# A three-block network on one core: expert results written per choice and summed on VectorE, first gathers ahead of a branch, unread matmuls in TensorE's waits

## The chip, the core and the metric

The kernel runs on one core of a Trainium2 chip. A core has five engines that each work through their own queue in order: TensorE (PE in the profile; its weight loads are PEld), VectorE (DVE), ScalarE (ACT), GpSimd (POOL) and SyncE (SP), which here only issues DMAs. Sixteen DMA engines move data between the chip's memory and the core. The metric is the device time of one execution in microseconds.

## What is computed

One call takes 512 latent tokens of width 1024 and 256 context tokens through a first block (a mixer of two gated linear recurrences, `hg` and `dn`, then a mixture of experts) and a second block (attention, a convolutional feed-forward, a spatial gating unit, a second feed-forward), all in float32. The change touches the mixture of experts most:

```python
def hierarchical_moe(h, w_group, b_group, w_expert, b_expert, w_gate, w_up, w_down):
    t = h.reshape(-1, h.shape[-1])
    ...
    g_idx = jnp.argmax(g_logits, axis=-1)              # one group of 4 experts
    ...
    top_v, top_i = lax.top_k(e_in_group, TOP_K_IN_GROUP)   # two experts of it
    top_w = jax.nn.softmax(top_v, axis=-1) * g_w
    ...
    y = jnp.zeros_like(t)
    for e in range(N_EXPERTS):                         # 16
        a = jax.nn.silu(t @ w_gate[e]) * (t @ w_up[e])
        y = y + gates[:, e:e + 1] * (a @ w_down[e])
    return y.reshape(h.shape)
```

Every token has exactly two experts, a first and a second choice, with weights from the softmax.

## The kernel before

**Precision.** Each float32 operand of a large matmul is split into a high and a low part (`split`: a cast on ScalarE makes the high part, a subtraction on VectorE the low part), and three matmuls are added up (`mm3`): high x high, low x high, high x low. In the trace a weight tile arrives as `wraw` or `wrawx` (1 MB, 128x2048), and its parts are `whi` and `wlo` (128x1024, two pieces to a load). `load_raw` issues the load on SyncE's queue when a buffer is free: two `wraw` and, in the expert phase, four `wrawx`. Of `whi` and `wlo` there are four buffers each.

**Order.** The program is written as Python generators that are advanced by turns; a scheduler then fixes the order of each engine's queue before the kernel runs. An engine that waits holds up all that stands behind it in its queue. `issue_after` ties instructions to stand behind a given one on its engine.

**Before the experts.** The recurrences end in `hg_core` and `dn_core`; each is followed by a projection. `out_proj` multiplies 1024 features in 4 blocks, adds the result to the residual stream `x`, and, in halves of 256 tokens, takes the mean square of the new rows (`msq`: matmuls with `ones`; `pow_half` on GpSimd; `spread`: transposes of `rrt`). It is used after the recurrences (`w_out`), after the attention, in the feed-forwards and in the gating unit.

**Experts.** `moe` writes the normed tokens to the table `hd` in memory, works out router logits, the two choices (`e12`, `mmask`) and each token's position in its expert's list (`posm`). `slot_onehot` makes one-hot matrices `soh` for two experts at a time; `slot_rows` multiplies them with `tw` (token number, weight high, weight low), copies the product to `srs`, transposes it and works out an index `sri` and a weight `srw` for each of an expert's 128 slots. An empty slot points behind the 512 tokens. `gather_slots` fetches the 128 token rows `xt` with an indirect DMA on GpSimd's queue, and `slots_feature` turns them into `xghi` and `xglo`. An expert (`hidden`, `turned`, `down`) needs 6 MB of weights: gate, up (contracted over 1024), then `esg` and `ea` (128x512), their transposes split into `eahi` and `ealo`, then down. The result `ey` is added into the rows of the table `ysd` by an indirect DMA that accumulates (`compute_op=ALU.add`). `ysd` has been zeroed earlier by five DMAs. Experts with more than 128 tokens are worked off in a loop inside a branch (`moe_overflow`), whose condition each engine loads; in the profiled data the branch is not taken. Before the branch six weight loads are issued (`early`). `moe` also gets `fill`, one step of the modulation vectors (eight matmuls, `L355`).

`moe_add` reads `ysd` back (`ys`, four loads of 128x4x256), transposes it, adds it to `x` with a gate and sums the squares. During this time TensorE has matmuls of the attention's projections on the context and latent tokens (`hthi`) to do.

## Time and profile before

| | us |
|---|---|
| median of three runs | 2380.99 (2379.49 to 2387.99) |
| the profiled execution, its own time | 2387.35 |
| span of that execution's trace | 2385.5 |
| TensorE busy | 2240.5 (94%) |
| VectorE busy | 1614.3 (68%) |
| ScalarE busy | 1200.8 (50%) |
| GpSimd busy | 620.3 (26%) |

The mean granted TensorE clock is 0.972 of full speed. The page's chain of waits, followed back from the last instruction, lies on TensorE for its matmuls for the most part. The busy time of an engine is an average over stages with different limits, and a matmul's end is modelled, so a busy TensorE isn't one at its peak. What a place is worth is read from the views of that place: which engine idled there, and what ended the idle time.

### The profile page before, as it was taken

The numbers are of one execution on the slowest core, as the hardware profiler recorded it, in microseconds if no ns is written. First come the engines' busy times: TensorE is split into PE (matmuls) and PEld (weight loads), VectorE is DVE, ScalarE is ACT, GpSimd is POOL, SyncE is SP. The second block draws the span as 40 slices with busy tenths as digits, with TensorE's granted clock in tenths as the row PEclk, the third lists the DMA queues.
The fourth block names the chain that finished last, engine by engine and source line by source line (L and its number), as shares of the span: only waits on it lengthen the run. The fifth ranks groups of instructions, "written<-read, shape, count | busy, mean of one in ns | idle before, by whom it ended". The sixth has DMA issues, their size and how long they took to land.

```text
span 2385.5 us, 33834 instructions
## 1 busy us (share of the span) xinstructions
PE 2240.5 (94%) x13058; PEld 1880.5 (79%) x13058; DVE 1614.3 (68%) x2545; ACT 1200.8 (50%) x1969; POOL 620.3 (26%) x470
## 2 busy tenths in 40 slices
PE   6998989989988899999999999999999999999998
PEld 3988977758875677778778878878888988888887
DVE  4777877778855888886857865896673445553553
ACT  4455644456754677776337763432342433432433
POOL 2133544345421111100441422332333001110111
PEclk9999999999999899999999999999999999999999
DMA  8564004151045799997210002656433222323321
GB/s 317 186 222 143 28 1 153 46 219 74 2 177 230 281 395 368 372 379 267 77 39 1 2 36 107 237 193 231 148 131 102 102 89 71 106 73 113 106 74 60
DMA packets 68405, 355.24 MB, mean 149 GB/s; under 512 B 8065, under 2 KB 12817, under 8 KB 37009
## 3 DMA queue, kind: packets, MB, share of 16 engines
q1 hardware_dynamic: 62752, 333.94, 38.0%
q0 software_dynamic: 5488, 19.11, 3.3%
q8 instruction: 104, 1.70, 0.3%
q14 instruction: 61, 0.49, 0.1%
HBM read 334.45 MB, written 19.40 MB: 148 GB/s over the span
## 4 chain that ended last, share of the span: by engine, by line
PE 43%; DVE 5%; issue 1%; ACT 1%; DMA 0%; POOL 0%; SPq 0%; POOLq 0%; DVEq 0%; ACTq 0%
PE mm L531 12%; PE mm L532 12%; PE mm L530 12%; PE sc L1598 2%; PE av L1751 1%; PE aux L1616 1%; DVE mva L385 1%; PE av L1742 1%; DVE smax L1605 1%; DVE wlo L273 1%; PE aux L1587 0%; DVE cy L1868 0%; PE aux L388 0%; DVE st L1577 0%; DVE alo L273 0%
## 5 line engine op out<-in xcount | busy, mean ns | idle before, releaser
L530 PE MATMUL mm<-hhi,whi 128*128 128x512 f32 (+1 forms) x1184 | 438.0, 375 | 10.3 <-ACT whi L270 5.3
L531 PE MATMUL mm<-hlo,whi 128*128 128x512 f32 (+1 forms) x1184 | 441.5, 374 | 2.9 <-DVE hlo L482 2.9
L532 PE MATMUL mm<-hhi,wlo 128*128 128x512 f32 (+1 forms) x1184 | 438.7, 372 | 0.0
L270 ACT CAST whi<-wraw 128x1024 fp32r<-128x1024 f32 (+1 forms) x240 | 246.3, 1041 | 300.1 <-PE mm L531 223.5
L273 DVE TENSOR_TENSOR wlo<-wraw,whi 128x1024 fp32r<-128x1024 f32 (+1 forms) x203 | 249.3, 1244 | 179.9 <-ACT whi L270 179.1
L273 DVE TENSOR_TENSOR wlo<-wrawx,whi 128x1024 fp32r<-128x1024 f32 x190 | 229.0, 1230 | 94.3 <-ACT whi L270 93.0
L270 ACT CAST whi<-wrawx 128x1024 fp32r<-128x1024 f32 (+1 forms) x210 | 215.0, 1048 | 154.2 <-PE mm L531 106.1
L530 PEld LDWEIGHTS mm<-hhi,whi 128*128 128x128 f32 x1184 | 224.8, 191 | 49.4 <-ACT whi L270 5.9
L531 PEld LDWEIGHTS mm<-hlo,whi 128*128 128x128 f32 x1184 | 225.9, 191 | 41.5 <-DVE hlo L482 3.3
L532 PEld LDWEIGHTS mm<-hhi,wlo 128*128 128x128 f32 x1184 | 225.4, 191 | 38.0 <-issue 0.2
L530 PE MATMUL mm<-whi,hhi 128*128 128x512 f32 (+1 forms) x640 | 218.2, 346 | 6.3 <-ACT hhi L481 2.3
L532 PE MATMUL mm<-whi,hlo 128*128 128x512 f32 (+1 forms) x640 | 219.9, 347 | 3.8 <-DVE hlo L482 3.7
L531 PE MATMUL mm<-wlo,hhi 128*128 128x512 f32 (+1 forms) x640 | 219.6, 345 | 0.5 <-DVE wlo L273 0.4
L385 DVE SCALAR_TENSOR_TENSOR mva<-mvr,cc_c,mva 128x512 f32<-128x512 f32 x154 | 156.6, 1017 | 3.4 <-DMA mvr<-in_w_mod_dram 1.2
L1878 POOL TENSOR_TENSOR cy<-cy,csg 128x512 f32<-128x512 f32 x44 | 64.7, 1472 | 348.0 <-DVE cy L1870 332.5
L531 PE MATMUL mm<-alo,whi 128*128 128x512 f32 (+1 forms) x396 | 145.0, 366 | 0.0
L530 PE MATMUL mm<-ahi,whi 128*128 128x512 f32 (+1 forms) x396 | 144.7, 367 | 0.0
L532 PE MATMUL mm<-ahi,wlo 128*128 128x512 f32 (+1 forms) x396 | 144.4, 366 | 0.0
L273 POOL TENSOR_TENSOR wlo<-wraw,whi 128x1024 fp32r<-128x1024 f32 (+1 forms) x37 | 90.1, 2434 | 203.7 <-ACT whi L270 195.4
L530 PEld LDWEIGHTS mm<-whi,hhi 128*128 128x128 f32 x640 | 125.1, 196 | 20.3 <-ACT hhi L481 2.8
L532 PEld LDWEIGHTS mm<-whi,hlo 128*128 128x128 f32 x640 | 124.9, 196 | 19.7 <-DVE hlo L482 6.2
L531 PEld LDWEIGHTS mm<-wlo,hhi 128*128 128x128 f32 x640 | 125.0, 196 | 14.4 <-DVE wlo L273 1.3
(548 smaller groups left out, 4672.4 us busy)
## 6 DMA issues: line engine op xcount, KB each, us to landing
wrawx<-in_w_down_dram SPq DMA_DIRECT2D x32, 1024.0 KB, 9.1
wrawx<-in_w_gate_dram SPq DMA_DIRECT2D x30, 1024.0 KB, 9.0
wraw<-in_w_up_dram SPq DMA_DIRECT2D x30, 1024.0 KB, 9.2
wraw<-in_ffn_w_up_dram SPq DMA_DIRECT2D x30, 1024.0 KB, 4.8
mvr<-in_ada_w_dram SPq DMA_DIRECT2D x56, 512.0 KB, 4.5
wraw<-in_ada_w_dram SPq DMA_DIRECT2D x20, 1024.0 KB, 4.9
wraw<-in_w_in_dram SPq DMA_DIRECT2D x18, 1024.0 KB, 6.9
mvr<-in_w_mod_dram SPq DMA_DIRECT2D x32, 512.0 KB, 4.4
```

The costliest lines, as they stand in the source:

```text
L270: nc.scalar.copy(hi, src)
L273: (lo_eng or nc.vector).tensor_sub(lo, src, hi.bitcast(F32))
L385: nc.vector.scalar_tensor_tensor(acc, raw[:, k, :], c, acc, op0=ALU.mult, op1=ALU.add)
L530: nc.tensor.matmul(out, ahi, bhi, start=start, stop=False)
L531: nc.tensor.matmul(out, ahi, blo, start=False, stop=False)
L532: nc.tensor.matmul(out, alo, bhi, start=False, stop=stop)
L1598: nc.tensor.matmul(s[:, a:a + n], qs[:, qt * P:qt * P + P], ks[i][:, a:a + n], start=i == 0, stop=i == 1)
L1605: nc.vector.tensor_reduce(m, s[:, :768], axis=AX.X, op=ALU.max, negate=True)
L1616: nc.tensor.transpose(tp[:, j, :], p[:, (a + j) * P:(a + j + 1) * P], self.ident)
L1742: nc.tensor.matmul(av[:, qt, :], pt[:, k, :], hd["v"][:, k, :], start=k == 0, stop=k == 5)
L1751: nc.tensor.matmul(av[j * 64:j * 64 + 64, qt, :], hd["v"][:, k, :], pt[:, k, :], start=k == 0, stop=k == 5, tile_position=(0, j * 64))
L1878: nc.gpsimd.tensor_mul(y, y, sg)
```

## The change

1. `ysd` grows from 640 to 1152 rows. A token's first choice is written to its own row and its second choice to the row 512 further on, so that no row is written twice. `tw` gets a fourth column with that row number, `slot_rows` gives two indices (`srix` for the gather, `sriy` for the scatter), the scatter is a plain write, and the zeroing DMAs go. `moe_add` loads both halves (eight loads, two buffers for each half) and adds them on VectorE.
2. The slot rows of experts 0 and 1 and their two gathers stand ahead of the overflow branch. The step `fill` stands behind the matmul `pre`, later than before.
3. Eight early weight loads instead of six, and six `wrawx` buffers instead of four; in the branch one buffer instead of two.
4. `warm` puts matmuls of `ones` with a constant, 128x512 in float32, into TensorE's queue. Nobody reads the result. There are four at the end of `hg_core`, four at the end of `dn_core`, two behind the second mean square in `out_proj` (after the recurrences, the attention, the first feed-forward and the gating unit), five ahead of the branch, four behind the sums of `moe_add`, and one and two in the first transposes of the attention.

```diff
+    def warm(self, behind, n):
+        with self.tc.issue_after(behind.ins):
+            p = self.ps.tile([P, 512], F32, name="aux", tag="aux")
+            for _ in range(n):
+                self.nc.tensor.matmul(p, self.ones, self.wide, start=True, stop=True)
...
@@ out_proj
                     bs.append(self.rstd(acc, ts.start // P, 2))
+                    if ts.start and not end:
+                        self.warm(self.summed, 2)
@@ hg_core, finish
+            if h == 3:
+                self.warm(out, 4)
             self.head_out(cp, po, ox[:, :, h * P:h * P + P])
@@ dn_chunk
-            mm4(p2, qk, vn)
+            out = mm4(p2, qk, vn)
+            if last and d:
+                self.warm(out, 4)
@@ down
-        nc.gpsimd.indirect_dma_start(out=ysd, out_offset=bass.IndirectOffsetOnAxis(ap=slot[0], axis=0), in_=y,
-                                     in_offset=None, compute_op=ALU.add)
+        nc.gpsimd.indirect_dma_start(out=ysd, out_offset=bass.IndirectOffsetOnAxis(ap=slot[1], axis=0), in_=y,
+                                     in_offset=None)
@@ slot_rows
-            row = pool.tile([P, 1], I32, name=name + "ri", bufs=8)
-            nc.vector.scalar_tensor_tensor(row, v[:, 0:1], float(T), w[:, 1:2], op0=ALU.add, op1=ALU.add)
+            row = [pool.tile([P, 1], I32, name=name + "ri" + c, bufs=8) for c in "xy"]
+            for c in range(2):
+                nc.vector.scalar_tensor_tensor(row[c], v[:, c:c + 1], float(T + c * T), w[:, 1:2], op0=ALU.add, op1=ALU.add)
@@ moe
-        for _ in fill:
-            pass
-        mvstack.close()
...
+        pre = nc.tensor.matmul(p[:, 1, :], self.ones, mf, start=True, stop=True)
+        with tc.issue_after(pre.ins):
+            for _ in fill:
+                pass
...
+        ty = rp.tile([P, 4, 16], F32, name="ty")
+        nc.vector.tensor_scalar(ty, e12[:, 1], float(T), float(-T), op0=ALU.mult, op1=ALU.add)
+        nc.vector.tensor_add(tw[:, :, :, 1], ty, self.c["tok"].unsqueeze(2).to_broadcast([P, 4, 16]))
...
+        two_rows(0)
+        gather(0)
+        gather(1)
+        self.warm(self.rowed, 5)
...
-                      for n, e in (("w_gate", 0), ("w_up", 0), ("w_gate", 1)) for k0 in (0, 4)]
+                      for n, e in (("w_gate", 0), ("w_up", 0), ("w_gate", 1), ("w_up", 1)) for k0 in (0, 4)]
         self.moe_overflow(dp, hd, ysd, tw, posm, ovl)
...
-            two_rows(0)
-            gather(0)
-            gather(1)
@@ moe_add
-        ys = pool.tile([P, 4, D], F32, name="ys")
-        for c in range(4):
-            nc.sync.dma_start(ys[:, :, c * 256:c * 256 + 256],
-                              ysd[0:T, c * 256:c * 256 + 256].rearrange("(j p) c -> p j c", p=P))
         for k in range(KD):
+            if k % 2 == 0:
+                ys = [pool.tile([P, 4, 256], F32, name=f"ys{c}", bufs=2) for c in range(2)]
+                for c in range(2):
+                    nc.sync.dma_start(ys[c], ysd[c * T:c * T + T, k * P:k * P + 256].rearrange("(j p) c -> p j c", p=P))
+                nc.vector.tensor_add(ys[0], ys[0], ys[1])
...
+        self.warm(self.summed, 4)
@@ the first block
-                for j in range(5):
-                    nc.sync.dma_start(ysd[j * P:j * P + P, :], z)
...
-            with K.phase(5, 0, 4):
+            with K.phase(5, 0, 6):
```

The scheduler's order moves with it. VectorE's queue around the fifth `srs` (the slot rows of experts 8 and 9; `xglo` is the low part of an expert's gathered rows; numbers tell buffers apart), before:

```order
L273 TENSOR_TENSOR xglo_9490<-aux_9491,xghi_9489 128x512
L273 TENSOR_TENSOR xglo_9490<-aux_9498,xghi_9489 128x512
L1325 COPY srs_9513<-aux_9508 6x256
L1245 TENSOR_TENSOR soh_9870<-cst_69,posm_8228 128x4x128
L273 TENSOR_TENSOR wlo_9447<-wrawx_9444,whi_9446 128x1024
L1245 TENSOR_TENSOR soh_9870<-cst_69,posm_8228 128x4x128
L1333 TENSOR_SCALAR srw_9518<-aux_9515,cst_69 128x1
L273 TENSOR_TENSOR wlo_9451<-wrawx_9444,whi_9450 128x1024
```

and with the change:

```order
L273 TENSOR_TENSOR xglo_9532<-aux_9533,xghi_9531 128x512
L273 TENSOR_TENSOR xglo_9532<-aux_9540,xghi_9531 128x512
L273 TENSOR_TENSOR wlo_9493<-wrawx_9486,whi_9492 128x1024
L273 TENSOR_TENSOR wlo_9512<-wrawx_9509,whi_9511 128x1024
L273 TENSOR_TENSOR wlo_9516<-wrawx_9509,whi_9515 128x1024
L1343 COPY srs_9555<-aux_9550 8x256
L1262 TENSOR_TENSOR soh_9916<-cst_69,posm_8243 128x4x128 x2
L273 TENSOR_TENSOR wlo_9577<-wrawx_9574,whi_9576 128x1024
L273 TENSOR_TENSOR wlo_9581<-wrawx_9574,whi_9580 128x1024
L273 TENSOR_TENSOR wlo_9605<-wraw_9602,whi_9604 128x1024
```

Three `wlo` that stood behind `srs` and `soh` now stand ahead of them.

TensorE's queue at the end of the attention's output projection, where `rrt` are the transposes of the second mean square and `hhi`, `hlo` the operands of the feed-forward that follows, before:

```order
L530 MATMUL mm_15270<-hhi512_15192,whi_15278 128x256
L530 MATMUL mm_15271<-hhi512_15192,whi_15278 128x256
L438 MATMUL aux_15187<-cst_69,rrt_15183 128x128 x2
L531 MATMUL mm_15270<-hlo512_15193,whi_15278 128x256
L532 MATMUL mm_15270<-hhi512_15192,wlo_15279 128x256
```

and with the change:

```order
L539 MATMUL mm_15357<-hhi512_15279,whi_15365 128x256
L539 MATMUL mm_15358<-hhi512_15279,whi_15365 128x256
L447 MATMUL aux_15271<-cst_69,rrt_15267 128x128 x2
L309 MATMUL aux_15274<-cst_69,ones_165 128x512 x2
L540 MATMUL mm_15357<-hlo512_15280,whi_15365 128x256
L541 MATMUL mm_15357<-hhi512_15279,wlo_15366 128x256
```

The unread pair (`cst,ones`) stands behind the transposes, and the matmuls on both sides are those of before.

VectorE's queue behind the overflow branch, around the first gathered rows' `xglo` (`soh` and `srs` behind it belong to the second and third pair of experts), before:

```order
L1333 TENSOR_SCALAR srw_8524<-aux_8516,cst_69 128x1
L1335 SCALAR_TENSOR_TENSOR sri_8526<-aux_8516,srw_8524 128x1
L1336 TENSOR_REDUCE srw_8524<-aux_8516 128x1
L273 TENSOR_TENSOR xglo_8534<-aux_8535,xghi_8533 128x512
L273 TENSOR_TENSOR xglo_8534<-aux_8542,xghi_8533 128x512
L1325 COPY srs_8557<-aux_8552 6x256
L1245 TENSOR_TENSOR soh_8767<-cst_69,posm_8228 128x4x128 x2
L273 TENSOR_TENSOR wlo_8633<-wrawx_8249,whi_8632 128x1024
```

and with the change, where the first pair's rows are already made ahead of the branch:

```order
L273 TENSOR_TENSOR wlo_8614<-wraw_8300,whi_8613 128x1024
L1343 COPY srs_8591<-aux_8586 8x256
L1262 TENSOR_TENSOR soh_8803<-cst_69,posm_8243 128x4x128 x2
L273 TENSOR_TENSOR wlo_8618<-wraw_8300,whi_8617 128x1024
L273 TENSOR_TENSOR wlo_8650<-wraw_8302,whi_8649 128x1024
L1351 TENSOR_SCALAR srw_8596<-aux_8593,cst_69 128x1
L273 TENSOR_TENSOR wlo_8654<-wraw_8302,whi_8653 128x1024
L273 TENSOR_TENSOR xglo_8568<-aux_8569,xghi_8567 128x512
L273 TENSOR_TENSOR xglo_8568<-aux_8576,xghi_8567 128x512
```

The second pair's `srs` and the third pair's `soh` stood behind `xglo` and now stand ahead of it, with four `wlo` around them.

## Rows read from the trace of the kernel before

**Rows 1.** By stage: us, busy of PE, PEld, DVE, ACT, POOL, PEclk, DMA share.

```profile
840.00:860.00 20.00, 20.00 (x98) 16.30 (x96) 19.38 (x28) 16.61 (x21) 4.11 (x3) 1.00 1.02 395
...
940.00:960.00 20.00, 19.18 (x91) 14.75 (x90) 18.00 (x24) 15.80 (x20) 2.58 (x2) 1.00 1.00 387
...
1478.00:1483.00 5.00, 5.00 (x25) 5.00 (x25) 3.69 (x11) 1.77 (x4) 0.70 (x1) 0.50 0.62 211
```

**Rows 2.** DMA 860 to 1056: packets, MB, share; a load, its median landing.

```profile
q1 hardware_dynamic: 8729, 63.61, 80.1%
...
wrawx<-in_w_gate_dram SPq DMA_DIRECT2D x20, 1024.0 KB, 9.0
```

**Rows 3.** DMA view of 780 to 789, where the software queue only gathers.

```profile
q0 software_dynamic: 288, 1.05, 29.6%
```

**Rows 4.** DMA view of 1100 to 1110, where the software queue only scatters.

```profile
q0 software_dynamic: 144, 0.52, 29.3%
```

**Rows 5.** Waits of ScalarE and TensorE, 789 to 1110: us, times, longest.

```profile
ACT whi L270 <- PE mm L532: 25.0, 44, 2.4
...
PE mm L531 <- DVE wlo L273: 6.6, 11, 1.4
```

**Rows 6.** Time order: a load on SyncE's queue, its first cast.

```profile
920.05 3.24 SPq L506 DMA_DIRECT2D wrawx<-in_w_gate_dram  x2
...
935.30 2.02 ACT L270 CAST whi<-wrawx 128x1024 fp32r<-128x1024 f32 x2
```

**Rows 7.** Time order, GpSimd: four of the 16 scatters.

```profile
841.32 1.62 POOL L1312 DMA_INDIRECT ysd<-ey,sri  x1 [10.10 <-ACT ey L1311]
...
877.38 1.58 POOL L1312 DMA_INDIRECT ysd<-ey,sri  x1 [15.74 <-ACT ey L1311]
...
957.79 2.98 POOL L1312 DMA_INDIRECT ysd<-ey,sri  x1 [17.41 <-ACT ey L1311]
...
997.12 1.77 POOL L1312 DMA_INDIRECT ysd<-ey,sri  x1 [17.42 <-ACT ey L1311]
```

**Rows 8.** Time order, VectorE: the fifth slot-row copy, idle before it bracketed.

```profile
879.49 0.41 DVE L1325 COPY srs<-aux 6x256 f32<-6x256 f32 x1 [2.52 <-PE aux L1322]
```

**Rows 9.** Time order, TensorE: first gathered rows, first matmul on `xglo`.

```profile
786.58 1.97 PE L1263 MATMUL aux<-cst,xt 128*128 128x128 f32 x8 [9.29 <-DMA xt<-hd,sri]
...
790.05 0.63 PE L532 MATMUL mm<-whi,xglo 128*128 128x512 f32 x1
```

**Rows 10.** Time order, VectorE: the routing behind the branch.

```profile
774.17 2.36 DVE L273 TENSOR_TENSOR wlo<-wraw,whi 128x1024 fp32r<-128x1024 f32 x2 [0.45 <-ACT whi L270]
...
776.78 1.27 DVE L1245 TENSOR_TENSOR soh<-cst,posm 128x512 fp32r<-128x512 f32 x2
```

**Rows 11.** Time order, TensorE: the end of `hg_core`.

```profile
362.81 0.79 PE L530 MATMUL mm<-hhi,whi 128*128 128x512 f32 x1 [5.27 <-ACT whi L270]
...
367.34 0.45 PE L530 MATMUL mm<-hhi,whi 128*128 128x512 f32 x1
```

**Rows 12.** Time order, TensorE: the end of `dn_core`.

```profile
689.94 1.19 PE L530 MATMUL mm<-hhi,whi 128*128 128x512 f32 x2 [4.09 <-POOL zero L2021]
...
695.16 0.39 PE L530 MATMUL mm<-hhi,whi 128*128 128x512 f32 x1
```

**Rows 13.** Time order, TensorE: two fp32 matmuls 128x512 at full clock.

```profile
62.66 1.02 PE L702 MATMUL aux<-clf,cst 128*128 128x512 f32 x2
...
63.52 1.02 PE L704 MATMUL aux<-clf,ones 128*128 128x512 f32 x2
```

**Rows 14.** Time order, TensorE: end of the attention's projection (one of three).

```profile
1477.67 0.58 PE L531 MATMUL mm<-hlo,whi 128*128 128x256 f32 x1 [1.39 <-DVE hlo L482]
...
1482.96 0.63 PE L438 MATMUL aux<-cst,rrt 128*128 128x128 f32 x2
...
1483.60 0.28 PE L532 MATMUL mm<-hhi,wlo 128*128 128x256 f32 x1
```

**Rows 15.** Time order, TensorE: behind the sums of `moe_add`.

```profile
1139.24 2.79 PE L438 MATMUL aux<-cst,rr 128*128 128x128 f32 x12 [3.56 <-DVE rr L463]
```

More of the change, by code (lines that the diff above doesn't have):

```diff
@@ L552, in gemm_feat, with out_proj @@
         return ps
-    def out_proj(self, w, ahis, alos, x, gate, last=True, lead=None):
+    def out_proj(self, w, ahis, alos, x, gate, last=True, lead=None, end=False):
         nk_all = len(ahis)
@@ L1017, in mm4 @@
             for h in range(4):
-                nc.tensor.matmul(p[:, h, :], l[:, h, :], r[:, h, :], start=start, stop=stop)
+                i = nc.tensor.matmul(p[:, h, :], l[:, h, :], r[:, h, :], start=start, stop=stop)
+            return i
         def tr4(p, src):
@@ L1586, in stack @@
                 for j in range(n):
-                    nc.tensor.matmul(p[:, j, :], st[:, j0 + j, b:b + 2, :], self.identr, start=True, stop=True)
+                    turned = nc.tensor.matmul(p[:, j, :], st[:, j0 + j, b:b + 2, :], self.identr, start=True, stop=True)
+                if first and j0 == 0:
+                    self.warm(turned, 1 + b)
                 (nc.vector.tensor_copy if b else nc.scalar.copy)(o[:, j0 * P:(j0 + n) * P],
@@ L1886, in conv_ffn @@
                     next(fill, None)
-            bs = self.out_proj(wd.rows(f0), ahis, alos, x, gate, half == 1)
+            bs = self.out_proj(wd.rows(f0), ahis, alos, x, gate, half == 1, end=l == 1)
         return bs
```

74 lines of the change are left out of this document (40 added, 34 removed).

## Prediction

> **What bounds the kernel now.** I read the table by stage first. While the experts run, the DMA share is 1.02 and 1.00, but TensorE is busy for 20.00 and 19.18 of 20 us, and VectorE for 19.38 and 18.00 [rows 1]: three resources stand close together, and the busy shares don't say which one ends last. The view of waits does. In the whole expert stage ScalarE's casts of weights wait for TensorE (44 times, 25.0 us) and TensorE waits for VectorE's `wlo` (11 times, 6.6 us) [rows 5]; no row of that view names a weight load. A single load shows why: the gate weights asked for at 920.05 are cast at 935.30 [rows 6], 15.25 us later, and such a load lands in a median of 9.0 us [rows 2], so it lies ready for some 6 us. The transfers run at their limit, but nobody waits for them.
>
> The scatter rows give the pace [rows 7]: 841.32 to 877.38 is 36.06 us for two experts, 18.03 each; 957.79 to 997.12 is 39.33, 19.67 each. Between them, 877.38 to 957.79 is 80.41 us for four experts. So the stage has a dense pace and a late one. The passage is one place: VectorE stands 2.52 us at the copy `srs` at 879.49, waiting for TensorE [rows 8], with the next `wlo` behind it; then TensorE stands for that `wlo`, and VectorE doesn't regain its lead.
>
> [...]
>
> **Part by part.** The sum is made against the profiled run, 2387.35 us, which is 6.36 above the median of the runs, 2380.99.
>
> *Plain scatter.* In a stretch with only gathers, 288 packets took 29.6% of sixteen engines for 9 us [rows 3]: 42.6 us of one engine, so for one gather (144 packets) 1.33 us of all sixteen. In a stretch with only accumulating scatters, 144 packets took 29.3% of 10 us [rows 4]: 2.93 us of all sixteen. A plain write of the same rows I price as the gather, so 1.6 us per expert go. The weights themselves are 80.1% of 196 us for 63.61 MB [rows 2], 2.47 us per MB, 15.5 for an expert's 6.29 MB. Demand is now 15.5+1.33+2.93 = 19.8 us per expert and then 18.2. At the late pace of 19.67 the loads already arrive in time, so there this gives nothing. At the dense pace of 18.03 today's demand would catch up with the kernel within a few experts; with 18.2 it hardly does. So the plain write doesn't bring speed, it allows the dense pace to last.
>
> *Order of VectorE in the experts.* Whether it lasts hangs on the rows of VectorE. Before the fifth `srs`, the one of 879.49, the order of before has no `wlo` between `xglo` and `srs`; the change has three, as before has ahead of the third and fourth `srs`, where the pace was dense. And `ea` is followed by four `wlo` ahead of `ealo` for six experts in a row in the change (before: five, with a break), by three for a seventh, and by two for nearly all of the rest, as in the late pace. So I take four more experts near the dense pace, 18.3 instead of 80.41/4 = 20.1: **-7.2 us**. If all of the next six with gathers follow it too, 6 x 1.37 = 8.2 more, -15.4; if a stall of the same kind only moves elsewhere, 0; with one stall more, 2.52 and the clock behind it, +3. VectorE's extra work, two index instructions per pair of experts, is some 0.3 us per pair and lies in its 2 us of slack [rows 1].
>
> *Early gathers.* Ahead of the branch the first gather doesn't stand behind the two pairs of `wlo` (2.36 us each, [rows 10]) and the branch, so it is issued some 5 us sooner and its rows land near 781.5 instead of 786.58 [rows 9]. But `xglo` now stands behind more on VectorE: one `wlo`, the second `srs` (which needs TensorE's transposes of the gathered rows and then the slot matmuls), `soh` x2, `wlo` x2, a small one, `wlo`. From rows gathered at 781.5: transposes and slot matmuls at full clock 1.5, `srs` 0.4, `soh` 1.27, three `wlo` 3.5, small ones 0.3, first half of `xglo` 0.7 [rows 8, 10]: 789.2; the five unread matmuls ahead of the branch (the first ones at half clock, an estimated 6 to 8 us from about 775.5) end at 781.5 to 783.5 and add up to 2. The first matmul that needs `xglo` stood at 790.05 [rows 9], after 1 us lost to the lower clock. I take **0**, range -3 to +3.
>
> *Unread matmuls in waits.* One costs 0.86 us at full clock (62.66 to 63.52, two records each, [rows 13]), so four are 3.44. At the end of `hg_core` TensorE waits 5.27 us and then does ten steps in 4.53 us (362.81 to 367.34, [rows 11]), twice the 0.227 of full clock. Four fit into the wait; the idle rest is 1.8 us. **-2.2** (bounds -2.3 and 0). At the end of `dn_core` it waits 4.09 and is at half clock from 689.94 to 695.16 [rows 12], worth 2.6; but 12 transposes of `oxh` that used to fill earlier waits now stand behind the four (eight cost 1.97 at half clock [rows 9], so twelve at full 1.5), which begins the projection about 0.9 us later: **-1.5** (-2.6 to +1).
>
> *At the ends of the projections* (attention, first feed-forward, gating unit) the pair stands behind the last `rrt` transposes. There TensorE doesn't wait: in the attention's case it comes back at 1477.67, works through matmuls at half clock, reaches `rrt` at 1482.96, and from 1483.60 on is at full clock [rows 14]. The pair stands where the half clock is just ending by itself, in front of dense work: 1.72 us, and 0.3 more for what still runs at half. **+2.0 each, +6.0** for the three; bounds 1.7 and 3.4 each (5.2 to 10.3). None below, since no low clock is left to shorten. [...] A fourth pair, at the output projection before the routing, costs the same 1.72, and there the eight matmuls of the moved modulation step leave the path (16 records, about as long): 0.
>
> *moe_add.* Eight loads instead of four, four additions of 128x1024 (1.2 us each, as a `wlo` [rows 10]), two buffers per half. Until the sums TensorE works on the attention's projections, which hides this. The first transposes of `ys` stood behind 115 of these matmuls, now behind 89: 26 x 0.227, some 6 us, less cover. The last scatter lands perhaps 2 us sooner; one more load of 512 KB and one addition stand ahead of the first transposes, 1.6+1.2. So TensorE may stand 1 to 3 us there: +1.5. The four unread matmuls fill the 3.56 us of 1139.24, where 12 transposes took 2.79 at half clock [rows 15]: -1.4. **0**, range -2 to +6. The zeroing DMAs that go stood in a projection that didn't wait for them: 0. Buffers six instead of four for loads that nobody waits for: 0.
>
> *Attention's start.* Three unread matmuls, 2.6 at full clock, in a stretch with waits: **-0.5** (-3 to +2.6).
>
> Sum: -7.2-2.2-1.5+6.0+0+0-0.5 = -5.4. Against the profiled run 2382.0; against the median **2375.6 us**.
>
> **Rivals.**
> *A. The dense pace holds through the experts* (the transfers were the real brake). For it: DMA share of 1.00 and more, the late pace just under today's demand of 19.8. Against: no wait for a load, 6 us of lead. -15.4 instead of -7.2: 2367.4. Chance 0.26.
> *B. Slower: the unread matmuls hold no clock and are simply added.* They stand in an in-order queue; if TensorE falls to half clock in spite of them, each costs 1.72. Then 3 x 3.4 at the projections, +2 at the routing, +2 at `dn_core`, +5 at the attention's start, +3.4 in `moe_add`: +22.6, less 7.2 of the experts: 2396. It decides wherever the wait is shorter than n x 1.72, 6.9 us for four: all the waits above. Against: four at full clock fit into 5.27 and 4.09. Chance 0.10.
> *C. VectorE starts late.* In expert 0 only two `wlo` now lie between `ea` and `ealo` (before three). If the late pace starts there, 1.4 more for each of four experts and nothing of the 7.2: 2388.2. Chance 0.08.
> *D. The early gather counts in full*, expert 0 begins 4.5 us sooner: 2371.1. Chance 0.08.
>
> **How the numbers follow.** The forecast has 0.48. The range reaches from A, with some more for the clock's places, 2359, to C, 2389; B is left out, and a little at both ends. About 0.5% (12 us, 2369 to 2393) is what a measurement of this kernel can tell from no change. Faster by more: A, and the forecast's own low end, 0.29. Slower by more: B, 0.10. Within: 0.61.
>
> **What would show it.** Right: scatters 18 to 18.5 us apart up to the eighth expert or so and 19.5 later; first `xglo` matmul near 790; no low clock after `hg_core` and `dn_core`; the low clock after the projections unchanged, with the unread pair behind `rrt` in a dense row; `ys` transposes earlier with a short wait. Wrong: if the experts keep 18.2 to the end (A), if the unread records are spaced 0.43 us and more than their wait (B), if scatters are 19.6 apart from the first (C).

## Result and the profile after

The change takes 2399.41 us (median, 2396.61 to 2400.04) where before takes 2382.47: 1.0066 times as long, 95% interval 1.0045 to 1.0087. The forecast was 2375.6, the range ended at 2389.

The profiled execution of the change took 2396.61 us (span 2394.8), 9.3 us of span more than that of before. That of before lay 4.9 above its median and that of the change 2.8 under its own, so the traces show 9.3 of the 16.9 us between the medians. First matmuls of TensorE divide the two:

| stretch | before | after | difference |
|---|---|---|---|
| start to the router's `mmask` | 767.0 | 766.3 | -0.7 |
| `mmask` to the first `ea` (expert 0) | 39.4 | 43.1 | +3.7 |
| first `ea` to the last `ealo` (expert 15) | 289.0 | 282.5 | -6.5 |
| last `ealo` to the first `rr` (`moe_add`) | 43.9 | 53.7 | +9.9 |
| `rr` to the first `mva` (attention) | 370.2 | 365.4 | -4.8 |
| `mva` (modulation sums of the first feed-forward) to that stage's first mean square | 343.9 | 350.6 | +6.7 |
| the rest | 532.3 | 533.2 | +0.9 |

Of the attention's -4.8, some 3 belong to the execution of before: four other kernels with no unread matmul there take 366.5 to 367.7. The two rows of the attention and of the first feed-forward also hang together: in the change the first `mva` stands 15 matmuls sooner, and these (0.227 us each, 3.4 in all) are counted one row later. From the last `rrt` of the attention to the next `rrt`, with the same matmuls in between, before takes 370.3 us and the change 375.0.

**Routing.** TensorE in the change (start, duration, engine, line, tiles; in brackets the idle time before and its releaser), where [rows 9] stood:

```profile
774.52 7.08 PE L309 MATMUL aux<-cst,ones 128*128 128x512 f32 x10
782.04 1.07 PE L1280 MATMUL aux<-cst,xt 128*128 128x128 f32 x8 [0.45 <-PEq L1549]
...
787.48 0.80 PE L539 MATMUL mm<-whi,xghi 128*128 128x512 f32 x1 [1.45 <-ACT xghi L270]
...
791.07 0.80 PE L541 MATMUL mm<-whi,xglo 128*128 128x512 f32 x1 [2.37 <-DVE xglo L273]
```

and ScalarE, in the change and then before:

```profile
781.76 1.28 ACT L270 ACT_TABLE_LOAD   x1 [10.08 <-PEq L1549]
783.06 3.88 ACT L270 CAST whi<-wraw 128x1024 fp32r<-128x1024 f32 x4
786.85 1.06 ACT L270 CAST xghi<-aux 128x512 fp32r<-128x512 f32 x2
```

```profile
771.80 1.28 ACT L270 ACT_TABLE_LOAD   x1 [5.46 <-DVEq L1518]
773.10 3.88 ACT L270 CAST whi<-wraw 128x1024 fp32r<-128x1024 f32 x4
```

The gathered rows are there early, `xt` is transposed 4.5 us sooner. But the unread five end at 781.60, and ScalarE's first step behind the branch starts 0.16 us later, released by TensorE's branch (`PEq`). Its casts of expert 0's weights begin 10 us later than before, `xghi` stands behind them, VectorE's `wlo` and `xglo` too. The greater part of the price is not these 0.16 us, but that the engines meet at the branch (5.3 of 9.2 us, experiment no_route5).

**Around moe_add.** What TensorE waited for from the last expert to `rr` (line, releaser: us, times, longest), then granted clock in two windows (us, busy PE, PEld, DVE, ACT, POOL, clock, DMA share, GB/s), then its last sums, where [rows 15] stood:

```profile
PE mm L539 <- ACT ey L1328: 3.5, 1, 3.5
PE sums L1539 <- ACT ysq L1537: 1.8, 2, 0.9
```

```profile
1091.00:1100.50 9.50, 6.04 (x32) 5.46 (x32) 3.57 (x4) 4.55 (x7) 0.96 (x1) 0.82 0.95 354
...
1139.60:1145.70 6.10, 6.10 (x9) 2.49 (x10) 0.99 (x6) 0.00 (x0) 2.04 (x2) 0.57 0.51 172
```

```profile
1135.98 1.05 PE L1539 MATMUL sums<-w,ysq 128*128 128x2 f32 x8 [0.85 <-ACT ysq L1537]
1137.93 1.80 PE L1539 MATMUL sums<-w,ysq 128*128 128x2 f32 x8 [0.90 <-ACT ysq L1537]
1139.59 6.29 PE L309 MATMUL aux<-cst,ones 128*128 128x512 f32 x8
1145.71 1.47 PE L447 MATMUL aux<-cst,rr 128*128 128x128 f32 x12
```

Behind the last expert TensorE stands 3.5 us for `ey` (before 0.9). It comes back at 1095.81 and runs at half clock from about 1097 to 1100.5 (granted clock 0.51; matmuls of 128x256 start 0.21 us apart there, and 0.12 on both sides). The last sums have no other work between them, TensorE waits twice, and the four unread matmuls take 6.3 us at clock 0.57, where before waited 3.56 [rows 15]. Why `ey` is late is seen on ScalarE:

```profile
1088.31 1.06 ACT L270 CAST whi<-wraw 128x1024 fp32r<-128x1024 f32 x1 [0.31 <-PE mm L541]
...
1092.39 1.04 ACT L270 CAST whi<-wraw 128x1024 fp32r<-128x1024 f32 x1 [0.31 <-PE mm L541]
1093.34 0.68 ACT L1327 ACTIVATE ey<-mm,srw 128x512 f32<-128x512 f32 x1
```

`ey` of expert 14 stands in the queue behind ten casts, of which the last ones wait one by one for a buffer that TensorE frees; before, it stood behind two.

**End of hg_core** ([rows 11]), in the change:

```profile
356.90 3.60 PE L309 MATMUL aux<-cst,ones 128*128 128x512 f32 x8
362.33 0.50 PE L539 MATMUL mm<-hhi,whi 128*128 128x512 f32 x1 [1.83 <-ACT whi L270]
...
364.31 0.63 PE L539 MATMUL mm<-hhi,whi 128*128 128x512 f32 x1
```

```profile
360.50:362.30 1.80, 0.00 (x1) 0.00 (x0) 0.66 (x3) 1.06 (x2) 0.00 (x0) 1.00 1.05 197
362.30:364.30 2.00, 1.75 (x4) 1.13 (x5) 1.99 (x2) 1.88 (x2) 0.00 (x0) 0.72 1.13 310
364.30:366.60 2.30, 2.30 (x7) 1.81 (x6) 1.51 (x2) 0.00 (x0) 0.00 (x0) 0.50 1.00 371
366.60:370.00 3.40, 3.40 (x16) 2.74 (x15) 0.00 (x0) 1.05 (x1) 0.82 (x1) 1.00 0.95 373
```

The four run at full clock (1.00 from 356.9 to 360.5) and shorten the wait to 1.83 us, as forecast. Then the clock falls all the same, while TensorE is at work again: 0.72, 0.50, and 1.00 from 366.6. Before, the low spell ended near 367.3 (0.50 from 362.8 on). From the last matmul of `hg_core` (on `hec`) to the 41st of the projection behind it, the change takes 17.0 us and before 17.1. It need not end like this: in raw4 (below), with the same four, the wait is 1.84 us, the clock stays up, and the distance is 15.5:

```profile
359.40:369.00 9.60, 9.38 (x39) 7.31 (x40) 3.44 (x3) 5.40 (x6) 2.77 (x2) 1.00 0.97 365
```

**First feed-forward.** TensorE's waits for `mva`, before and after, from 1483 (1487) to the end of the stage:

```profile
PE aux L388 <- DVE mva L385: 4.7, 4, 1.6
```

```profile
PE aux L397 <- DVE mva L394: 6.8, 4, 2.1
```

The transposes of `mva` stand up to 37 matmuls sooner in TensorE's queue than before. Nothing of the change's text touches them: the scheduler moved them.

### The profile page after: what moved, and what is told of

Read it like the earlier page. It is cut to its first block, busy times and chain, and to the rows that moved or that the text cites. A ratio compares the mean times of both kernels' runs of the same rounds, so it can differ in the third digit from the quotient of the medians.

```text
span 2394.8 us, 33978 instructions
## 1 busy us (share of the span) xinstructions
PE 2264.6 (95%) x13114; PEld 1886.0 (79%) x13114; DVE 1619.3 (68%) x2567; ACT 1202.3 (50%) x1969; POOL 607.6 (25%) x470
## 4 chain that ended last, share of the span: by engine, by line
PE 44%; DVE 4%; issue 1%; ACT 1%; POOL 0%; DMA 0%; SPq 0%; POOLq 0%; DVEq 0%; ACTq 0%
PE mm L540 13%; PE mm L541 12%; PE mm L539 12%; PE sc L1631 2%; PE aux L1649 1%; PE av L1784 1%; PE av L1775 1%; DVE mva L394 1%; DVE smax L1638 1%; DVE wlo L273 0%; PE aux L1618 0%; ACT pexp L1640 0%; PE aux L397 0%; PE aux L309 0%; PE aux L1861 0%
## 5 line engine op out<-in xcount | busy, mean ns | idle before, releaser
L270 ACT CAST whi<-wraw 128x1024 fp32r<-128x1024 f32 (+1 forms) x224 | 230.7, 1040 | 286.6 <-PE mm L540 214.2
L273 DVE TENSOR_TENSOR wlo<-wraw,whi 128x1024 fp32r<-128x1024 f32 (+1 forms) x187 | 229.9, 1241 | 176.4 <-ACT whi L270 175.2
L273 DVE TENSOR_TENSOR wlo<-wrawx,whi 128x1024 fp32r<-128x1024 f32 (+1 forms) x206 | 247.2, 1230 | 109.5 <-ACT whi L270 108.5
L270 ACT CAST whi<-wrawx 128x1024 fp32r<-128x1024 f32 (+1 forms) x226 | 231.3, 1049 | 169.2 <-PE mm L540 110.6
```

Of the source, the lines that this page charges most:

```text
L270: nc.scalar.copy(hi, src)
L273: (lo_eng or nc.vector).tensor_sub(lo, src, hi.bitcast(F32))
```

## Experiments

The theories that the expectations name: **1**, all engines meet at the branch, and the five unread matmuls bring TensorE there last. **2**, the two further `wrawx` buffers change ScalarE's order at the last experts. **3**, the double-buffered loads and additions bring the last sums late. **4**, the order of the first feed-forward costs some 5 us. **5**, the other unread matmuls hold no clock where they stand. Their rivals are the prediction's terms and its rival B (unread matmuls are simply added).

"Part 1" to "part 4" are the numbers of the section on the change. Each ratio is to the kernel before in the same series (medians there 2383.0 to 2383.8). The measure used below for the routing goes from the last `rrt` transposes ahead of the router to the first `ea`: 57.4 us before, 60.9 in the change.

### The unread matmuls, and the five ahead of the branch

**no_unread**: all of part 4 left out.

```diff
-                        self.warm(self.summed, 2)
-                self.warm(out, 4)
-                self.warm(out, 4)
-        self.warm(self.rowed, 5)
-        self.warm(self.summed, 4)
-                    self.warm(turned, 1 + b)
```

> All 28 unread matmuls of the change are left out (hg_core, dn_core, projection ends, ahead of the branch, behind the sums, first transposes of the attention); the rest is the change. In the trace of the change ScalarE's first cast of an expert weight starts at 783.06, when TensorE has ended the five unread matmuls ahead of the branch (781.60), and before it started at 773.10. Theory 1 (the engines meet at the branch, so the five hold up everyone): without them ScalarE's casts start near 776.5, the first matmul on xghi near 784 instead of 787.5, about 3 to 4 us gained; behind the sums of moe_add some 2.4 us are gained (the four run 6.3 us at half clock in a wait that was 3.6), and at hg_core and dn_core about 3 us are lost again. Together 2393 to 2397 us against 2399.4 of the change. Rival B (unread matmuls are simply added, at 0.86 us and more each): 28 x 0.86 = 24 us less, 2375 or under. As in the prediction (they hold the clock in waits, the pairs cost): 2399 to 2400, no change.

2385.2 us, 1.0005 (0.9995 to 1.0015): 14 us under the change, more than theory 1 had. Routing 50.4 us.

**no_route5**

```diff
-        self.warm(self.rowed, 5)
```

> Only the five unread matmuls ahead of the overflow branch are left out. Theory 1 (the engines meet at the branch): ScalarE's first cast of an expert weight starts near 776.5 instead of 783.06 and TensorE's first matmul on xghi near 784 instead of 787.48; expert 0 begins 3 to 4 us sooner: 2395 to 2396 us against 2399.4. Rival (the loss at expert 0 comes from the longer row on VectorE ahead of xglo, second srs, two soh and wlo): the first matmul on xglo stays near 791 and the time near 2399. The scheduler also moves rows inside the experts when the five are gone; if that weighs more, the start of expert 0 moves as theory 1 says and the pace of the experts takes the gain back or adds to it, up to 5 us either way.

2392.36 us, 1.0043 (1.0030 to 1.0056), 7 under the change. First matmul on `xghi` 782.2, on `xglo` 783.9; routing 51.7, 9.2 less than the change. Theory 1 holds, with a larger size, but the meeting is only a part of it. ScalarE, VectorE and the clock of the first matmuls, here and then in the change:

```profile
776.21 1.28 ACT L270 ACT_TABLE_LOAD   x1 [5.32 <-DVEq L1549]
783.13 1.28 DVE L273 TENSOR_TENSOR xglo<-aux,xghi 128x512 fp32r<-128x512 f32 x2
784.33 0.40 DVE L1343 COPY srs<-aux 8x256 f32<-8x256 f32 x1
784.20:790.20 6.00, 6.00 (x32) 4.89 (x31) 5.44 (x8) 3.85 (x5) 0.00 (x0) 1.00 0.71 261
```

```profile
785.28 0.41 DVE L1343 COPY srs<-aux 8x256 f32<-8x256 f32 x1
790.35 1.27 DVE L273 TENSOR_TENSOR xglo<-aux,xghi 128x512 fp32r<-128x512 f32 x2
787.40:795.50 8.10, 5.65 (x12) 3.87 (x13) 6.05 (x14) 1.55 (x3) 0.94 (x1) 0.50 0.79 299
```

Without the five VectorE is the last to come to the branch (`DVEq`). Counted from the last `rrt` ahead of the router, ScalarE's first step comes 27.8 us later instead of 33.2: 5.3 for the meeting. The first matmul on `xglo` gains 7.0; the further 1.7 go with VectorE's queue, where the scheduler, without the five, puts `xglo` ahead of `srs` and `soh`. Expert 0's first matmuls are at full clock from 784.2, where the change has half clock until 795.5: with that it is 9.2.

**part2_five**: the five added to a kernel without them (part2_three, below). The scheduler moves `srs` and `soh` ahead of the first `xglo` with it, as in the change.

```diff
         gather(1)
+        self.warm(self.rowed, 5)
```

> The kernel with part 2 and the three unread matmuls of the attention's start (part2_three), plus the five unread matmuls ahead of the branch, and nothing else; the order of the other instructions stays as good as the same. Theory 1 (all engines go on behind the branch only when TensorE has come there, so the five stand on everyone's path): the first matmul on ea comes 4 us later behind mmask than without them if the five run at full clock, and 9 us later if they run at half clock; 2381 to 2386 us against 2377.3. Rival (they fit into the wait for the gathered rows, as the prediction has it, at most +2): 2377 to 2379.

2381.40 us, 0.9988 (0.9977 to 0.9999), 4.1 above part2_three; routing 57.2 against 50.9. Of these 6.3 us ScalarE's first step behind the branch accounts for 2.9; the place of `xglo` and half clock at expert 0's start (0.50 from 785.3 to 793.4) make up the rest. In three kernels, the five, and ScalarE's first step behind the branch:

| kernel | the five take | granted clock | they end | ScalarE goes on | routing |
|---|---|---|---|---|---|
| the change | 7.08 | 0.64 | 781.60 | 781.76 | 60.9 |
| part2_five | 6.25 | 0.72 | 779.45 | 779.62 | 57.2 |
| accumulate (below) | 4.56 | 1.00 | 775.44 | 775.61 | 55.3 |

The rows of accumulate, TensorE and ScalarE:

```profile
770.88 4.56 PE L309 MATMUL aux<-cst,ones 128*128 128x512 f32 x10
```

```profile
775.61 1.28 ACT L270 ACT_TABLE_LOAD   x1 [6.94 <-PEq L1548]
776.90 3.89 ACT L270 CAST whi<-wraw 128x1024 fp32r<-128x1024 f32 x4
```

The same five take 4.56 us at full clock and 7.08 where the clock is low for the greater part; ScalarE waits for them either way.

### The other unread matmuls

**no_sums4**

```diff
-        self.warm(self.summed, 4)
```

> The change without the four unread matmuls behind the sums of moe_add; the rest of the order stays. Theory 5 (TensorE is at half clock when it comes to them, so they take 6.3 us in a wait of 3.6, and the faster transposes of rr behind them only run into the next wait): 2 to 3 us less, 2396 to 2398 against 2399.4. The prediction (they fill the wait and give 1.4): 2401.

2400.5 us, 1.0064 (1.0045 to 1.0084): no gain in the median; the runs lie between 2391.6 and 2401.6. In the trace the distance from the last of the sums' matmuls to `rr` falls from 6.33 to 3.91 us:

```profile
1139.44 1.38 PE L1539 MATMUL sums<-w,ysq 128*128 128x2 f32 x8 [0.90 <-ACT ysq L1537]
1144.38 2.79 PE L447 MATMUL aux<-cst,rr 128*128 128x128 f32 x12 [3.56 <-DVE rr L472]
```

`rr` is at half clock again (2.79 us, as before, where the granted clock was 0.50, instead of 1.47 at 1.00), but it is 2.4 earlier, and 2.4 earlier the kernel reaches the attention and its output projection. That is theory 5's place and size, and the opposite of the prediction's -1.4; the medians don't resolve it. In the other traces with the four the distance is 4.8 to 7.3, in those without them 3.8 to 3.9 (4.8 in part2_3_three).

**no_hgdn**

```diff
-                self.warm(out, 4)
-                self.warm(out, 4)
```

> The change without the four unread matmuls at the end of hg_core and the four at the end of dn_core. The prediction's terms, -2.2 and -1.5, would be lost: 2403. Theory 5 (they hold no clock there: in the change's trace TensorE still stands 1.8 us behind the four and then does the same steps at half clock, and behind dn_core what they gain the held-up transposes of oxh lose): 0, up to 1 either way there. The order of the first feed-forward becomes that of the other runs, which is 2 us slower than that of the change: 2399 to 2402 in all; what tells the two apart is the distance from the last matmul of hg_core and dn_core to the first of the projection behind it.

2399.49 us, 1.0066 (1.0050 to 1.0081). From the last `hec` matmul of `hg_core` to the last `rrt` ahead of the router, which takes in both places, it is 391.9 us without, 391.8 with, 391.8 before. Theory 5 holds: together they are worth nothing that shows. Behind `dn_core` the four even bring the last `rrt` 2.4 us later (66.0 instead of 63.6 behind the last matmul of the recurrence, on `dnvn`), while the stretch ahead of that matmul is 2.5 shorter.

**no_pairs**

```diff
-                    if ts.start and not end:
-                        self.warm(self.summed, 2)
```

> The change without the four unread pairs behind the second mean square of a projection (after the recurrences, the attention, the first feed-forward, the gating unit). The prediction charges 2.0 for each of three and 1.7 for the first: 2391.7. Theory 5, from the runs so far with and without all unread matmuls: the pair after the recurrences costs 1.8, that after the first feed-forward 1.5, that after the attention gives 1.0 back since half clock stood there, that in the gating unit 0: 2 us less, and 2 us more by the order of the first feed-forward: 2398 to 2400.

2394.57 us, 1.0046 (1.0028 to 1.0064), 4.8 less than the change, and more than theory 5 had. After the attention, without the pair and then with it in the change:

```profile
1482.84 0.38 PE L447 MATMUL aux<-cst,rrt 128*128 128x128 f32 x2
...
1483.18 0.28 PE L541 MATMUL mm<-hhi,wlo 128*128 128x256 f32 x1
```

```profile
1486.65 0.38 PE L447 MATMUL aux<-cst,rrt 128*128 128x128 f32 x2
1486.87 1.88 PE L309 MATMUL aux<-cst,ones 128*128 128x512 f32 x4
...
1488.70 0.28 PE L541 MATMUL mm<-hhi,wlo 128*128 128x256 f32 x1
```

From `rrt` to the same matmul on `hhi,wlo` it is 0.34 us without and 2.05 with: the pair is simply added, 1.7 us. It is the same in the first feed-forward, 1.7 (1.93 to 0.21), and in the gating unit, where from the second `rrt` to the next one the six kernels with the pair take 358.9 to 359.3 us and the ten without 357.2 to 357.4. After the recurrences it is 1.5 (24.90 to 23.41). That is 6.6 in all, where theory 5 let the attention's pair give 1.0 back: from `rrt` to the first `mva` the change is indeed 1.0 faster (24.44 to 25.46), but because `mva` stands behind 12 matmuls fewer there.

### The parts, one upon the other

**part1_alone**: part 1 on before. In the change's text this is parts 2 to 4 undone.

```diff
-        two_rows(0)
-        gather(0)
-        gather(1)
...
             w = self.weights
+            two_rows(0)
+            gather(0)
+            gather(1)
...
-            with K.phase(5, 0, 6):
+            with K.phase(5, 0, 4):
```

> Only part 1 of the change on top of before: plain scatter into 1152 rows, no zeroing, eight loads and four additions in moe_add. No early gathers, four buffers, no unread matmuls. TensorE's order ends here, as in the run with four buffers (raw4), with 52 transposes and sums in a row behind the last of the attention's matmuls, where before has 28 among them. Theory 3 (the plain write costs at moe_add, by that order): from the last matmul on ealo to the last of the sums some 6 us more than before's 40.0, as in raw4 (46.4), which nothing else takes back: 2387 to 2391 us against 2383.2 of before. The prediction's working (no bound in the transfers, moe_add 0, a denser row of VectorE in the experts -7): 2376. Rival (the scatter itself was the brake of the experts): the experts' pace is 18.3 to the end and 2370.

2386.51 us, 1.0014 (1.0004 to 1.0024). Last `ealo` to `rr` 50.4 us (before 43.9): as theory 3 has it. The last small matmuls, and the clock over them:

```profile
1130.76 3.57 PE L1541 MATMUL sums<-w,ysq 128*128 128x2 f32 x16 [0.71 <-ACT ysq L1539]
...
1136.85 3.57 PE L1541 MATMUL sums<-w,ysq 128*128 128x2 f32 x16 [0.71 <-ACT ysq L1539]
1143.98 2.80 PE L447 MATMUL aux<-cst,rr 128*128 128x128 f32 x12 [3.56 <-DVE rr L472]
```

```profile
1130.00:1140.10 10.10, 8.68 (x41) 8.23 (x40) 3.38 (x4) 2.52 (x4) 0.00 (x0) 0.50 0.15 57
```

**part1_2**: part 2 on top of it.

```diff
+        two_rows(0)
+        gather(0)
+        gather(1)
...
-            two_rows(0)
-            gather(0)
-            gather(1)
```

> Parts 1 and 2 on top of before: plain scatter with its moe_add, and the first gathers ahead of the branch; four buffers, no unread matmuls. Theory 1 (the early gathers are worth 6 us at expert 0 as soon as no unread matmuls keep TensorE from the branch): the first matmul on ea comes 6 us sooner behind the router's mmask than before (33.2 instead of 39.4 us), so this kernel lies 6 us under the one with part 1 alone: 2381 to 2385. Rival (the gain at expert 0 is taken back by waits for weight loads, which are not asked for sooner): the two are equal.

2377.68 us, 0.9975 (0.9965 to 0.9985): 8.8 under part1_alone. Routing 53.0 against 57.8.

**part2_alone**: part 2 on before, that is part1_2 with part 1 undone.

```diff
-        nc.gpsimd.indirect_dma_start(out=ysd, out_offset=bass.IndirectOffsetOnAxis(ap=slot[1], axis=0), in_=y,
-                                     in_offset=None)
+        nc.gpsimd.indirect_dma_start(out=ysd, out_offset=bass.IndirectOffsetOnAxis(ap=slot[0], axis=0), in_=y,
+                                     in_offset=None, compute_op=ALU.add)
```

> Part 2 alone on top of before: the first gathers ahead of the branch (with the index column that nothing but the scheduler sees); accumulating scatter, four buffers, no unread matmuls. The order at the last expert and in moe_add is that of before, but in the first feed-forward the transposes of mva stand up to 31 matmuls sooner on TensorE than before, as in the change and in all runs so far. Theory 1 with theory 4 (that order costs 5 us: TensorE waits twice for VectorE, 1.4 and 2.2 us, and has half clock behind it): -6 at expert 0 and +5 in the feed-forward, 2381 to 2384 against 2383.2 of before. If the feed-forward's order costs nothing: 2377.

2381.54 us, 0.9993 (0.9983 to 1.0004). Last `ealo` to `rr` is 43.8 as before; first `ea` to last `ealo` 286.8, with plain scatters (part1_2) 286.8 too. The first feed-forward takes 348.2 instead of 343.9.

**part2_three**

```diff
                 if first and j0 == 0:
+                    self.warm(turned, 1 + b)
```

> Part 2 on top of before, and of the unread matmuls only the three in the first transposes of the attention. Here the order of the first feed-forward is that of before. Theories 1 and 4: -6 at expert 0, nothing lost in the feed-forward, 0 to -2 at the attention's start: 2375 to 2378 us against 2383.2 of before, and 5 us under the kernel with part 2 alone. Rival (the feed-forward's loss has another cause than the order): equal to the kernel with part 2 alone.

2377.33 us, 0.9970 (0.9958 to 0.9982), faster than both kernels. Feed-forward 343.9, with the order of before; part2_alone, then part2_three:

```profile
PE aux L397 <- DVE mva L394: 6.7, 6, 2.2
```

```profile
PE aux L397 <- DVE mva L394: 4.8, 4, 1.6
```

**part1_2_three**

```diff
                 if first and j0 == 0:
+                    self.warm(turned, 1 + b)
```

> Parts 1 and 2 and the three unread matmuls in the first transposes of the attention. By the three alone the order of the first feed-forward becomes the one in which the transposes of mva stand up to 31 matmuls sooner. Theory 4 (this order costs 4 to 6 us there, whatever else is in the kernel): 2381 to 2384 us against 2377.7 without the three, and from the first mva to the mean square of the feed-forward's output 348 to 350 us instead of 343.8. Rival (its loss in the other runs had to do with unread matmuls or accumulating scatters): 2377 to 2378 and 344.

2385.83 us, 1.0011 (1.0002 to 1.0021), 8.2 above part1_2; feed-forward 349.8 against 343.8, TensorE's waits for `mva` 8.2 instead of 4.7 us. So the same three unread matmuls turn the order for the better in one kernel and for the worse in another: theory 4 holds, and what hangs on it is 4 to 8 us by the medians. From `rrt` to `rrt` it is 3.6 us (370.0 to 373.6, part2_three and part2_alone) and 5.3 (369.9 to 375.2). All sixteen traces fall in with this: the six with the order of before take 343.8 to 343.9 us from the first `mva` to the mean square, the ten others 348.2 to 351.4.

### The two further buffers, and the plain write in the change

**raw4**: part 3 undone.

```diff
-                      for n, e in (("w_gate", 0), ("w_up", 0), ("w_gate", 1), ("w_up", 1)) for k0 in (0, 4)]
+                      for n, e in (("w_gate", 0), ("w_up", 0), ("w_gate", 1)) for k0 in (0, 4)]
...
-            with K.phase(5, 0, 6):
+            with K.phase(5, 0, 4):
```

> Part 3 of the change is undone: six early weight loads instead of eight, four wrawx buffers instead of six, two in the branch instead of one. In the change TensorE stands 3.46 us for ScalarE's ey behind the last expert and then does 16 matmuls at half clock; on ScalarE the two ey of expert 14 stand behind ten casts in a row there, and before behind two. With four buffers the order of ScalarE is that of before again. Theory 2 (the two further buffers let the scheduler put casts ahead of the result copies ey, and this is the greater part of what the time around moe_add lost): the wait of 3.46 falls to 1 us or less, the half clock behind it goes, about 4 us gained there. If the same buffers carry the faster pace of experts 4 to 8 in the change (18.3 us), those go back to 19.5 and lose 5 to 8 us: then 2399 to 2404 in all; if they don't, 2395. Rival (buffers for loads that nobody waits for change nothing, as the prediction has it): the wait stays, 2399.

2401.87 us, 1.0082 (1.0067 to 1.0097). The wait for `ey` falls to 0.9 us, as theory 2 has it; the experts go back to 287.1 us (first `ea` to last `ealo`), and last `ealo` to `rr` stays at 52.7, since TensorE now has 52 transposes and sums in a row at the end, as in part1_alone, where the granted clock over them was 0.50; here it was 0.86 on the mean from 1084.0 to 1145.8. That the wait was the greater part of `moe_add`'s loss is wrong.

**accumulate**: part 1 undone in the change; the scatter as in part2_alone, and

```diff
-                nc.vector.tensor_add(ys[0], ys[0], ys[1])
...
+        ys = pool.tile([P, 4, D], F32, name="ys")
+        for c in range(4):
+            nc.sync.dma_start(ys[:, :, c * 256:c * 256 + 256],
```

> Part 1 of the change is undone: the scatter accumulates into 640 zeroed rows again, and moe_add loads four pieces of one table without an addition; parts 2 to 4 stay. From the last matmul on ealo (1091.97) to the last of the sums of squares the change takes 47.4 us and before takes 40.0. Theory 3 (the eight double-buffered loads and the additions bring the last sums late, so that they stand behind all other work of TensorE): the distance falls by 2 to 4 us, 2395 to 2397 us. Theory 2 (ScalarE's order at the last expert, which stays here): the 3.46 us for ey stay, and the distance falls by no more than 1; 2398 to 2400. The prediction's terms (plain scatter no bound in itself, moe_add near 0) give no change either; if the accumulating scatters slow the loads enough to be waited for, the experts take 5 us and more longer: 2404.

2400.39 us, 1.0074 (1.0061 to 1.0088). Last `ealo` to the last sums 48.0 us, as in the change (47.4): theory 3 is not what makes `moe_add` slow here. TensorE waits 6.3 us for the first `ys` load: with six buffers their transposes stand behind 74 of the projections' matmuls, before behind 115.

**part2_3_three**: part 3 on part2_three, with the same order of the feed-forward.

```diff
-            with K.phase(5, 0, 4):
+            with K.phase(5, 0, 6):
```

> The kernel with part 2 and the three unread matmuls (part2_three), plus part 3: eight early weight loads, six wrawx buffers. The order of the first feed-forward stays that of before, so part 3 stands alone against that kernel. Theory 2 (the two further buffers give the experts some 5 us and take more back behind them): from the first matmul on ea to the last on ealo 282 to 283 us instead of 287, then TensorE stands 3.5 instead of 0.9 us for ey and some 6 us for the first rows of ys, whose transposes the order now puts behind 74 of the projections' matmuls instead of 115; from the last ealo to rr 51 to 52 us instead of 45. In all 2379 to 2381 against 2377.3. Rival (as the prediction has it, buffers for loads that nobody waits for change nothing): 2377. Rival (part 3 costs 7 us, as the medians of the kernels with parts 1 and 2 and with parts 1 to 3 say): 2384.

2379.12 us, 0.9976 (0.9964 to 0.9988), not to be told from part2_three. Experts 282.2 instead of 286.8, last `ealo` to `rr` 52.7 instead of 45.2: part 3 gives 4.6 and takes 7.4. TensorE's waits there:

```profile
PE aux L1533 <- DMA ys<-ysd: 5.5, 1, 5.5
PE mm L539 <- ACT ey L1328: 3.5, 1, 3.5
```

One upon the other, in ratios to before (no_unread is parts 1 to 3): part 1 +0.14%, part 2 -0.39%, part 3 +0.30% (with the feed-forward's order, which comes with it there), the unread matmuls +0.61%.

## Why the prediction was wrong

- **The five ahead of the branch** are the part of the change that the prediction had most wrong. "Add up to 2" counted them in TensorE's queue only. ScalarE goes on behind the branch when the last engine has come there (0.16 to 0.17 us behind TensorE's last matmul in the three kernels of the table), and its casts, which the sum didn't name, had used this time before. No_route5 puts the price of the five at 7 us in the median and 9.2 in the trace; of the latter 5.3 are the meeting, the rest is the place of `xglo` on VectorE and the clock at expert 0's start.
- **Rival B** has the direction and the nearest time, 2396. Its mechanism is right for the pairs, which are added whole, and for the four behind the sums. The time is near by luck: B's "+2 at the routing" is too small and its "+5 at the attention's start" was 0, and it had nothing for the rest of `moe_add` or for the first feed-forward. All 28 cost 14 us (no_unread), not 22.6.
- **Early gathers, 0.** Without the five they give 4.4 (part1_2) to 6.5 us (part2_three): rival D's 4.5 is right for them, and the five take it away.
- **moe_add, 0** (-2 to +6): +9.9, the largest miss of a single place. Besides the four unread matmuls (2.4) there are two sources: the order that the further buffers bring (late `ey`, then `ys` ahead of its loads: +7.4 in part2_3_three against part2_three) and the small matmuls in a row that part 1 brings (+6.6 in part1_alone). They don't add up; with both, in no_unread, it is 53.1 against 43.9. "Buffers six instead of four: 0" was read from loads that nobody waits for. The buffers change ScalarE's order. The reading itself wasn't complete either: the view of [rows 5] does name a weight load, the first one of the attention's, behind the last expert, where the range of that view ends:

```profile
ACT whi L270 <- DMA wrawx<-in_attn_w_in_dram: 2.8, 1, 2.8
```

- The prediction names no row for the 1.6 us of one more load of 512 KB in `moe_add`. The 63.61 MB in 196 us of [rows 2] give it; at the 2.47 us per MB of the weights it would be 1.3, which changes nothing in the sum.
- **The first feed-forward** has no term in the prediction. Its row shows +6.7, of which 3.4 is work moved over from the row above. The order costs the other 3.3: from `rrt` to `rrt` the change takes 375.0 us, 1.7 of it for the unread pair, and kernels with the order of before take 370.0. I had compared the orders where the diff stands, and took the rest as it was.
- **Experts, -7.2**: -6.5 measured, and that the two are near is luck. The stall at the fifth `srs` goes: expert 4 to 5 takes 22.1 us before, 19.7 in part1_alone and part2_three. That gives 2.4 and nothing follows from it. The rest comes with the six buffers, which the prediction set at 0: in the change the distance from one expert's `ea` to the next is 16.1 to 18.8 us from expert 1 to 8, and 22.8 from 8 to 9.
- **Plain scatter is no bound**: right, 286.8 us for the experts with either. "It allows the dense pace to last": wrong, with four buffers both go at the late pace after the fifth expert, and with six the accumulating scatter keeps the faster pace too (283.1 in accumulate, 282.5 in the change).
- **hg_core -2.2, dn_core -1.5**: 0 together (no_hgdn). I took the low clock of [rows 11, 12] to follow from the length of the wait, which no run shows; with the wait at the end of `hg_core` cut to 1.83 us it came none the less in the change (0.50 from 364.3 to 366.6), and with 1.84 us it stayed away in raw4 (1.00).
- **Pairs, +6.0 for three**: right. The traces give 1.7 each, 5.2 in all, the lower of the bounds, so the pairs are simply added and the 0.3 for a remaining low clock was not seen. The fourth costs 1.5, and was set against the moved `fill`.
- **Attention's start, -0.5**: 0 (`rr` to the last `sc` 272.06 in part2_three, 272.04 without the three in part2_alone); through the order of the feed-forward the three weigh up to 8.

What stays open: by the medians the five (7.0) and the pairs (4.8), and by the trace the sums (2.4), make up the 14.2 us of the unread matmuls. By the traces alone the five and the pairs are dearer (9.2 and 6.6), and executions of one kernel differ too (the twelve of part2_3_three: mean granted clock 0.975 to 0.983, 2371.82 to 2383.80 us), so this sum is no proof that nothing else is in it. Nor was it tried what makes the order of the first feed-forward turn.

## What to carry to other kernels

Filler on TensorE ahead of a branch that all engines take held up ScalarE's first step behind it by 5.3 us here (no_route5): count what each engine does first behind such a branch. Where a scheduler sets the order, compare the orders of the whole program, also far from the edit; here the order of a stage that no edit touches cost 3 to 5 us. Take a bundle apart: part 2 with three of the 28 unread matmuls gave a kernel 0.3% faster than before.

## What the runs showed of the hardware

- ScalarE's first step behind the branch starts 0.16 to 0.17 us after TensorE's last matmul ahead of it, in the three kernels of the table.
- The same five unread matmuls took 4.56, 6.25 and 7.08 us in three kernels, at a granted clock of 1.00, 0.72 and 0.64.
- At the end of `hg_core` four unread matmuls at clock 1.00 and a wait of 1.83 us didn't prevent the low spell in the change; it came when TensorE was at work again (0.72 from 362.3 to 364.3, 0.50 from 364.3 to 366.6). In raw4, with a wait of 1.84, it stayed away (1.00 from 359.4 to 369.0).
- An unread pair of 128x512 in a dense row, at a granted clock of 1.00 (1486.87 to 1488.75 in the change), cost 1.7 us, its own time (rows of no_pairs).
- In part1_alone the granted clock was 0.50 from 1130 to 1140, where TensorE did transposes of 128x128 and sums of two columns.
- In before the granted clock was 0.50 from 362.8 to 367.3 and from 689.94 to 695.16 ([rows 11, 12]), from 786.58 to 788.55 ([rows 9]) and from 1139.2 to 1142.0 ([rows 15]). It was 1.00 from 62.6 to 64.0 ([rows 13]). In the dense row at 840, which [rows 1] has at full clock, matmuls of 128x512 start 0.227 us apart.
